# Leading bank, pinned weight splits, wide rotated chunks, and GpSimd lo parts in a two-block transformer

## The chip, the cores and the metric

The kernel runs on one core of a Trainium2 chip. The metric is the device time of one execution in microseconds, the median of several timed runs. One more execution was profiled; all profile rows come from it.

## The reference, cut to what matters

The input x has 256 tokens of width 1024. A first block (four token mixers, gates, an MLP of 4096) is followed by a retention layer with an FFN and by a native-sparse-attention (NSA) layer with an FFN. All of it is in float32. The change touches the products around these formulas:

```python
# retention, per head h (4 heads, q and k 256 wide, v 512 wide)
q, k = rotate_pairs(q, cos, sin), rotate_pairs(k, cos, sin) * (dk ** -0.5)
scores = einsum('bhid,bhjd->bhij', qc, kc) * intra_decay
o = einsum('bhij,bhje->bhie', scores, vc) + ...        # the state of the chunk before
o = o * rsqrt(mean(o * o) + eps);  out = (o * silu(g)) @ w_out
# NSA, shared keys and values
kc = silu(blocks(k_c + pe) @ w1_k) @ w2_k              # 15 blocks per group, hidden 256, width 64
vc = silu(blocks(v_c + pe) @ w1_v) @ w2_v
gate = sigmoid((x @ w_in)[..., 1024:])                 # 16 heads x 3 branches
o = gate0 * compressed + gate1 * selected + gate2 * window
# every layer
h = h + rms_norm(mixed);  normed = rms_norm(h);  h = h + rms_norm(swiglu_ffn(normed))
```

## The kernel before

Float32 products are made of three float32r products. A weight of 128x1024 (a *half*) is loaded into a raw tile (4 of them), ScalarE writes its rounded copy whi (L234), VectorE the rest, wlo = raw - whi (L237); activations are split the same way. `mm3` (L249 to L251) adds hi.hi, hi.lo and lo.hi in PSUM. Six buffers (WSP) hold halves, more where a stage opens a pool for its last ones. `ws_wide` (L274, L276) makes the same sum in two products: whi against x's hi and lo side by side (512 columns), and wlo against x's hi (256 columns); ScalarE then copies the second part (L277) and VectorE adds the first (L278). `ws_chunk` makes it with mm3 at 256 columns.

A layer ends in `project_back` (w_out, w_down, w_ro, w_fo, w_no): for each of two token halves t two PSUM banks of 512 columns are summed over all weight halves. The last six halves (last = 3 chunks of two) are *held*: t = 0 runs bank 0 over all of them and then bank 1, then `residual(0)` and `nxt.a(0)` (normalization of the rows: L406, L411, L414, a power on GpSimd at L416, L193 on VectorE and L194 on ScalarE) are written; then t = 1 runs, with `nxt.b(0)` (transposes L436, then hi and lo of the inputs at L209 and L210) ahead of the last held half. For w_out and w_no nk is 8, so six of the eight halves are held. The next layer starts with `an_groups`: eight halves (two groups of four), each used for t = 0 and, after `nxt.b(1)`, for t = 1; their wlo is made in two pieces of 512.

Tiles are placed and instructions ordered by a scheduler: on each engine it takes the first instruction in the order of the code that is ready by its own estimate, so a weight split far down can stand ahead of a residual, and products can change places. `issue_after` adds an edge that keeps an instruction behind a given one on the same engine.

Retention projects q and k of each head with ws_chunk (w_rqk, eight chunks), rotates them from PSUM (L1127 to L1130, the last sum on GpSimd), takes the scores of head h-1 after the q chunk of head h, and then for each of four groups runs `gates` (w_rg by `an_steps`, four halves) and `outputs`: at and v stay float32 there (L1164, L1166). NSA runs a list of steps, NSA_ORDER: K and Q are halves of the key and query projections, I0/I1 the inputs of the compressed keys and values (xs), H0/H1 their hidden layer (w_ck1, w_cv1, four halves each, L1366 and L1368), T, C the second layer, G and B the gate products, S and U the scores. `keep_queries` makes lo parts of the queries (L1338); `cmp_values` writes the values four times below each other (L1417) by 32 products of 32 rows.

## Time and profile before

| | us |
|---|---|
| median of 3 timed runs | 1207.35 (1204.04 to 1207.77) |
| profiled execution | 1208.24 |
| its span, first to last instruction | 1206.46 |

| engine | busy us | share |
|---|---|---|
| TensorE products | 1184.8 | 98% |
| TensorE weight loads | 1014.4 | 84% |
| VectorE | 806.3 | 67% |
| ScalarE | 662.9 | 55% |
| GpSimd | 80.8 | 7% |

PE is TensorE, PEld its weight loads, DVE VectorE, ACT ScalarE, POOL GpSimd, SP the queue that issues the loads. Products are pipelined and the ends of their records are modelled: records of 0.28 us that start 0.12 us apart take 0.12 us each. PEclk is the share of full speed that TensorE was granted. A float32 product shows as two records. "<-" behind an idle time names what ended it.

### The profile page before, as it was taken

The page shows a single profiled execution, that of the slowest core. Times are in us where ns is not written, and L with a number is a line of the kernel's source. Part 1 is how long each engine was busy: PE and PEld are TensorE (multiplying, and loading weights), DVE is VectorE, ACT ScalarE, POOL GpSimd, SP SyncE. Part 2 cuts the span into 40 slices and gives each one's busy share as a digit, 9 for nine tenths or more (in the row PEclk, how much of TensorE's full clock was granted, in tenths as well). Part 3 has the DMA queues.
Part 4 walks back from the last instruction along what each step waited for, and adds up shares of the span by engine and source line. Part 5 has one row for each costly group of instructions (what it writes and reads, how often), then busy time and mean ns, then how long its engine had stood idle before and what let it go on. Part 6 is the DMA issues. An engine that isn't in the chain of part 4 may idle for free.

```text
span 1206.5 us, 18129 instructions
## 1 busy us (share of the span) xinstructions
PE 1184.8 (98%) x6848; PEld 1014.4 (84%) x6848; DVE 806.3 (67%) x1413; ACT 662.9 (55%) x1148; POOL 80.8 (7%) x87
## 2 busy tenths in 40 slices
PE   8999999999999998999999999999999999999997
PEld 6999889887888887899878888888889877888886
DVE  7757877667746667557456665657778967655663
ACT  5545765655644454543555554556567876645561
POOL 1000001200000000012000000000100530000000
PEclk8999999999999999999999999999999999999999
DMA  7654454536455565554546355556655226555560
GB/s 239 196 175 158 140 191 158 175 126 230 161 192 187 191 208 181 177 194 158 166 148 213 120 192 189 192 185 212 209 194 179 72 70 205 179 189 186 189 205 35
DMA packets 60775, 210.11 MB, mean 174 GB/s; under 512 B 7120, under 2 KB 9808, under 8 KB 60560
## 3 DMA queue, kind: packets, MB, share of 16 engines
q1 hardware_dynamic: 60688, 208.95, 53.0%
q8 instruction: 54, 0.88, 0.3%
q14 instruction: 33, 0.27, 0.1%
HBM read 207.84 MB, written 1.08 MB: 173 GB/s over the span
## 4 chain that ended last, share of the span: by engine, by line
PE 82%; DVE 7%; DMA 5%; ACT 3%; issue 1%; POOL 0%; SPq 0%; DVEq 0%; POOLq 0%; ACTq 0%
PE b L274 19%; PE b L249 15%; PE b L251 15%; PE b L250 15%; PE b L276 9%; DVE wlo L237 3%; ACT whi L234 1%; PE b L436 1%; DMA raw<-w_up 1%; DMA raw<-w_no 1%; DMA raw<-w_rv 1%; PE b L1536 1%; DMA raw<-w_ck 1%; DMA wng<-w_ng 1%; ACT s L1503 1%
## 5 line engine op out<-in xcount | busy, mean ns | idle before, releaser
L237 DVE TENSOR_TENSOR wlo<-raw,whi 128x1024 fp32r<-128x1024 f32 (+3 forms) x432 | 470.9, 1103 | 265.1 <-ACT whi L234 262.2
L234 ACT ACTIVATE whi<-raw 128x1024 fp32r<-128x1024 f32 (+1 forms) x384 | 401.6, 1050 | 383.6 <-issue 116.5
L274 PE MATMUL b<-x,whi 128*128 128x512 f32 x1024 | 362.7, 398 | 0.0
L276 PE MATMUL b<-x,wlo 128*128 128x256 f32 x1024 | 286.3, 280 | 0.0
L249 PE MATMUL b<-whi,x 128*128 128x512 f32 (+1 forms) x720 | 283.9, 395 | 1.8 <-ACT x L209 1.0
L250 PE MATMUL b<-wlo,x 128*128 128x512 f32 (+1 forms) x720 | 280.7, 390 | 1.0 <-DVE wlo L237 0.8
L251 PE MATMUL b<-whi,x 128*128 128x512 f32 (+1 forms) x720 | 279.8, 390 | 0.6 <-DVE x L210 0.6
L274 PEld LDWEIGHTS b<-x,whi 128*128 128x128 f32 x1024 | 192.2, 188 | 45.9 <-issue 0.3
L276 PEld LDWEIGHTS b<-x,wlo 128*128 128x128 f32 x1024 | 193.1, 189 | 0.9
L249 PEld LDWEIGHTS b<-whi,x 128*128 128x128 f32 x720 | 136.1, 189 | 34.5 <-ACT x L209 4.3
L251 PEld LDWEIGHTS b<-whi,x 128*128 128x128 f32 x720 | 136.3, 189 | 29.9 <-DVE x L210 1.3
L250 PEld LDWEIGHTS b<-wlo,x 128*128 128x128 f32 x720 | 136.4, 189 | 28.7 <-DVE wlo L237 1.9
L249 PE MATMUL b<-x,whi 128*128 128x256 f32 x480 | 137.6, 287 | 0.0
L251 PE MATMUL b<-x,wlo 128*128 128x256 f32 x480 | 135.5, 282 | 0.4 <-DVE wlo L237 0.4
L250 PE MATMUL b<-x,whi 128*128 128x256 f32 x480 | 135.4, 282 | 0.0
L249 PEld LDWEIGHTS b<-x,whi 128*128 128x128 f32 x480 | 91.5, 191 | 2.1 <-issue 1.5
L251 PEld LDWEIGHTS b<-x,wlo 128*128 128x128 f32 x480 | 91.5, 191 | 0.6 <-DVE wlo L237 0.6
L250 PEld LDWEIGHTS b<-x,whi 128*128 128x128 f32 x480 | 91.6, 191 | 0.1
L416 POOL TENSOR_TENSOR rstd<-ms,mhalf 128x1 f32<-128x1 f32 x22 | 13.8, 626 | 686.5 <-DVE ms L414 686.5
L210 DVE SCALAR_TENSOR_TENSOR x<-b,gc,x 128x128 fp32r<-128x128 f32 x112 | 36.7, 348 | 20.2 <-ACT x L209 18.3
L209 ACT ACTIVATE x<-b,gc 128x128 fp32r<-128x128 f32 x112 | 37.9, 367 | 21.7 <-PE b L436 16.5
L1503 ACT ACTIVATE s<-s,nm 128x128 f32<-128x128 f32 (+1 forms) x64 | 28.2, 444 | 2.6 <-DVE rz L1507 1.4
(277 smaller groups left out, 1014.8 us busy)
## 6 DMA issues: line engine op xcount, KB each, us to landing
raw<-w_fi SPq DMA_DIRECT2D x88, 512.0 KB, 4.5
raw<-w_fo SPq DMA_DIRECT2D x44, 512.0 KB, 4.5
raw<-w_gate SPq DMA_DIRECT2D x32, 512.0 KB, 4.2
raw<-w_up SPq DMA_DIRECT2D x32, 512.0 KB, 3.9
raw<-w_down SPq DMA_DIRECT2D x32, 512.0 KB, 3.9
raw<-w_qk SPq DMA_DIRECT2D x24, 512.0 KB, 4.1
raw<-w_rv SPq DMA_DIRECT2D x16, 512.0 KB, 4.8
raw<-w_rqk SPq DMA_DIRECT2D x16, 512.0 KB, 4.5
```

The costliest lines, as they stand in the source:

```text
L209: k.nc.scalar.activation(hi, ps[:, j, :], AF.Copy, scale=g)
L210: k.nc.vector.scalar_tensor_tensor(lo, ps[:, j, :], g, hi.bitcast(F32), op0=OP.mult, op1=OP.subtract)
L234: nc.scalar.activation(hi[:, :n], r, AF.Copy)
L237: nc.vector.tensor_tensor(lo[:, c], r[:, c], hi[:, c].bitcast(F32), op=OP.subtract)
L249: mm(out, lhs[0], rhs[0], start=start, stop=False)
L250: mm(out, lhs[0], rhs[1], start=False, stop=False)
L251: mm(out, lhs[1], rhs[0], start=False, stop=stop)
L274: mm(ps.rearrange("p a t -> p (a t)"), half[0][:, s], x[2][:, k].rearrange("p a t -> p (a t)"), start=k == 0, stop=False)
L276: mm(ps[:, 0], half[1][:, s], x[0][:, k, :], start=False, stop=k == KT - 1)
L416: nc.gpsimd.tensor_tensor(r, ms, self.mhalf[:, :1], op=OP.pow)
L436: self.nc.tensor.transpose(ps[:, j, :], src[:, j * 128:(j + 1) * 128], self.ident)
L1503: nc.scalar.activation(s[:, a, i, :], s[:, a, i, :], AF.Exp, bias=nm[:, a, i:i + 1], scale=-1.0, accum_out=z[:, a, i:i + 1])
```

## The change

- `each_half` can make wlo on another engine; `cmp_hidden` makes the eight halves of the compressed layers on GpSimd, and `keep_queries` the lo parts of the queries.
- `an_groups` queues the splits of its third and later halves behind the last ScalarE and VectorE instructions of `nxt.a(0)` (*the pins*: `lasts`, `queued`, `rows_done`).
- `project_back`: where nk is 8, t = 0 (and t = 1 of a last layer) takes bank 0 of one held half ahead and then alternates the two banks.
- Retention: w_rqk by ws_wide, rotation from SBUF, the scores of head h-1 after the k chunk, those of the last head within the first gates; at and v are split into hi and lo (in the tiles of the rotation) and `outputs` multiplies by mm3.
- NSA: the gate weights are split after `an_groups`, the gate products come before H0, and `cmp_values` makes its four copies by 8 products, from an hT that GpSimd has copied four times.

```diff
-NSA_ORDER = ("Q0 K0 I0 H0 Q0 Q0 G I1 Q1 Q1 Q1 T0 K1 B C0 K1 K1 H1 K0 K0 "
+NSA_ORDER = ("Q0 K0 I0 G H0 Q0 Q0 I1 Q1 Q1 Q1 T0 K1 B C0 K1 K1 H1 K0 K0 "
...
-    def each_half(self, name, i, width=2048, pools=None, pieces=1):
+    def each_half(self, name, i, width=2048, pools=None, pieces=1, lo_on=None):
...
-                nc.vector.tensor_tensor(lo[:, c], r[:, c], hi[:, c].bitcast(F32), op=OP.subtract)
+                (lo_on or nc.vector).tensor_tensor(lo[:, c], r[:, c], hi[:, c].bitcast(F32), op=OP.subtract)
...
                 for j in range(4):
+                    queued = self.queued(self.rows_done if len(hs) > 1 else ())
                     if j % 2 == 0:
                         own = {s: pool for s in range(2) if len(hs) + s + extra >= 4 * len(groups)}
                         chunk = self.each_half(name, 2 * g + j // 2, 4 * n, own, 2)
-                    hs.append((i, 2 * j, next(chunk)))
+                    with queued:
+                        hs.append((i, 2 * j, next(chunk)))
...
+            lead = min(len(held), 1 if nk == KT else len(held))
             for t in range(2):
-                for banks in ((0,), (1,)) if t == 0 or not nxt else ((0, 1),):
-                    for a in held[:-1]:
-                        self.as_t(accs[t], *a, t, banks)
-                    if t and nxt:
+                if t == 0 or not nxt:
+                    order = [(i, 0) for i in range(lead)]
+                    for i in range(len(held)):
+                        order += [(i + lead, 0)] * (i + lead < len(held)) + [(i, 1)]
+                else:
+                    order = [(i, n) for i in range(len(held)) for n in range(2)]
+                for i, n in order:
+                    if t and nxt and (i, n) == (len(held) - 1, 0):
                         nxt.b(0)
-                    self.as_t(accs[t], *held[-1], t, banks)
+                    self.as_t(accs[t], *held[i], t, (n,))
                 residual(t, accs[t])
                 if nxt:
                     nxt.a(t)
+                    if t == 0:
+                        self.rows_done = self.lasts()
...
+    def lasts(self):
+
+        order = list(reversed(self.nc.cur_bb.bb.instructions))
+        return [next(i for i in order if i.engine == e.engine) for e in (self.nc.scalar, self.nc.vector)]
+
+    def queued(self, instructions):
+
+        es = ExitStack()
+        for i in instructions:
+            es.enter_context(self.tc.issue_after(i))
+        return es
...
-            def rotated(s, ps):
-                a = tp.tile([128, 2, T], F32, tag=f"rot{s}", name="rot")
+            def rotated(s, i):
+                a = self.ws_wide("w_rqk", i, xin, tp.tile([128, 2, T], F32, tag=f"rot{s}", name="rot"))
                 b = tp.tile([128, 2, T], F32, tag="rotb", name="rotb")
-                nc.vector.tensor_tensor(a, ps, cs, op=OP.mult)
                 for j in range(2):
-                    nc.vector.tensor_tensor(b[:, j, :], ps[:, 1 - j, :], sn[:, j, :], op=OP.mult)
+                    nc.vector.tensor_tensor(b[:, j, :], a[:, 1 - j, :], sn[:, j, :], op=OP.mult)
+                nc.vector.tensor_tensor(a, a, cs, op=OP.mult)
                 nc.gpsimd.tensor_tensor(a, a, b, op=OP.add)
...
-                    rot.append(rotated(s, self.ws_chunk("w_rqk", 2 * h + s, xin)))
-                    if s == 0 and qk:
+                    rot.append(rotated(s, 2 * h + s))
+                    if s == 1 and qk:
                         scores(h - 1, *qk)
...
+                    steps += 1
+                    if steps == 2 and g == 0:
+                        scores(3, *qk)
+                    if steps == (3 if g == 0 else 1):
+                        src = [v[:, t, g * 512:(g + 1) * 512] for t in range(2)] + [at[:, g, :]]
+                        for tag, x in zip(("rot0", "rot1", "rotb"), src):
+                            hl = [tp.tile([128, 2, T], F32, tag=tag, name=tag).rearrange("p a t -> p (a t)").bitcast(F32R)
+                                  [:, :x.shape[1]] for _ in range(2)]
+                            self.split(*hl, x)
+                            parts.append(hl)
+                return sg, parts
...
-                    mm(p, at[:, g, t * 128:t * 128 + 128], v[:, 0, vs], start=True, stop=t == 0)
+                    self.mm3(p, [x[:, t * 128:t * 128 + 128] for x in w], v0, True, t == 0)
                     if t:
-                        mm(p, at[:, g, T:384], v[:, 1, vs], start=False, stop=True)
+                        self.mm3(p, [x[:, T:384] for x in w], v1, False, True)
...
-            wg = tp.tile([128, KT, 96], F32R, name="wg")
-            self.split(wg[:, :, :48], wg[:, :, 48:], raw.rearrange("p (k c) -> p k c", k=KT))
...
+            wg = tp.tile([128, KT, 96], F32R, name="wg")
+            self.split(wg[:, :, :48], wg[:, :, 48:], raw.rearrange("p (k c) -> p k c", k=KT))
...
-                    nc.vector.tensor_tensor(lo, q[half[a], :, 128:], hi.bitcast(F32), op=OP.subtract)
+                    nc.gpsimd.tensor_tensor(lo, q[half[a], :, 128:], hi.bitcast(F32), op=OP.subtract)
...
-                    for u, (hi, lo) in enumerate(self.halves("w_c" + "kv"[s] + "1", c)):
+                    for u, (hi, lo) in enumerate(self.halves("w_c" + "kv"[s] + "1", c, lo_on=nc.gpsimd)):
...
+                for r in range(1, nr):
+                    nc.gpsimd.tensor_copy(hT[:, :, :, r, :15], hT[:, :, :, 0, :15])
...
-                for r in range(4):
-                    for g in range(4):
-                        for k in range(2):
-                            mm(p[r * 32:r * 32 + 32, g, :], hT[:, k, g, :], w2[:, 1, k, :], start=k == 0, stop=k == 1)
+                for g in range(4):
+                    for k in range(2):
+                        mm(p[:, g, :], hT[:, k, g].rearrange("p r n -> p (r n)"), w2[:, 1, k, :], start=k == 0,
+                           stop=k == 1)
```

## Rows read from the trace of the kernel before

**Rows 1.** Page of the profile: TensorE's busy time, share of the span, instructions.

```profile
PE 1184.8 (98%) x6848; PEld 1014.4 (84%) x6848; DVE 806.3 (67%) x1413; ACT 662.9 (55%) x1148; POOL 80.8 (7%) x87
```

**Rows 2.** TensorE timeline, 256-column and wide products: start, length, engine, line, shape.

```profile
559.99 0.28 PE L249 MATMUL b<-x,whi 128*128 128x256 f32 x1
...
560.35 0.28 PE L249 MATMUL b<-x,whi 128*128 128x256 f32 x1
...
729.98 0.40 PE L274 MATMUL b<-x,whi 128*128 128x512 f32 x1
...
730.33 0.39 PE L274 MATMUL b<-x,whi 128*128 128x512 f32 x1
```

**Rows 3.** TensorE timeline, outputs of one retention group and what follows.

```profile
587.91 1.88 PE L1164 MATMUL b<-v,at 128*128 128x512 f32 x4
...
590.72 0.39 PE L250 MATMUL b<-wlo,x 128*128 128x512 f32 x1
```

**Rows 4.** Timeline of TensorE and VectorE near the end of w_no.

```profile
995.80 0.47 PE L249 MATMUL b<-whi,x 128*128 128x512 f32 x1
...
997.04 0.50 PE L250 MATMUL b<-wlo,x 128*128 128x512 f32 x1 [0.76 <-DVE wlo L237]
...
998.54 1.22 DVE L237 TENSOR_TENSOR wlo<-raw,whi 128x1024 fp32r<-128x1024 f32 x1 [1.56 <-ACT whi L234]
...
998.56 1.03 PE L249 MATMUL b<-whi,x 128*128 128x512 f32 x2 [0.79 <-ACT whi L234]
...
1000.68 0.63 PE L250 MATMUL b<-wlo,x 128*128 128x512 f32 x1
```

**Rows 5.** TensorE timeline, held halves of w_out.

```profile
277.78 0.74 PE L249 MATMUL b<-whi,mx 128*128 128x512 f32 x2 [0.75 <-ACT whi L234]
```

**Rows 6.** Windows: length, PE, PEld, DVE, ACT, POOL busy, granted clock, DMA, GB/s.

```profile
477.30:480.00 2.70, 2.70 (x11) 2.51 (x12) 0.69 (x3) 1.06 (x4) 0.00 (x0) 0.50 0.00 0
...
999.00:1001.00 2.00, 2.00 (x6) 1.62 (x5) 1.75 (x3) 0.98 (x1) 0.00 (x0) 0.50 0.80 266
```

**Rows 7.** Timelines of VectorE and TensorE between w_down and retention.

```profile
469.98 1.29 DVE L237 TENSOR_TENSOR wlo<-raw,whi 128x512 fp32r<-128x512 f32 x2 [2.81 <-ACT whi L234]
...
477.28 1.94 PE L436 MATMUL b<-cm,xn 128*128 128x128 f32 x8 [3.34 <-DVE xn L193]
```

**Rows 8.** TensorE timeline, first products of the MLP.

```profile
292.38 0.50 PE L251 MATMUL b<-whi,x 128*128 128x512 f32 x1 [0.59 <-DVE x L210]
```

**Rows 9.** Windows from one normalization to the next transposes: retention, FFN, NSA, FFN.

```profile
477.14:489.03 11.89, 11.75 (x50) 9.95 (x51) 7.17 (x19) 5.50 (x15) 1.10 (x2) 0.88 0.30 110
676.02:689.38 13.36, 13.36 (x63) 10.73 (x62) 9.19 (x23) 7.49 (x19) 1.40 (x2) 1.00 0.17 43
863.04:874.98 11.94, 11.92 (x58) 9.59 (x56) 8.79 (x26) 7.74 (x24) 3.45 (x9) 1.00 0.59 164
1011.72:1024.31 12.59, 12.31 (x59) 9.79 (x58) 10.82 (x27) 8.78 (x20) 1.39 (x2) 1.00 0.48 162
```

**Rows 10.** Timelines of ScalarE and TensorE in NSA: gate split, first of H0.

```profile
877.60 0.52 ACT L242 ACTIVATE wg<-wng 128x384 fp32r<-128x384 f32 x1 [0.78 <-DMA wng<-w_ng]
...
903.18 0.38 PE L1366 MATMUL b<-whi,xs 128*120 128x256 f32 x1 [0.62 <-DVE xs L243]
```

**Rows 11.** Timelines of TensorE and GpSimd: the values, the first scores' multiplies.

```profile
937.73 3.18 PE L1417 MATMUL b<-w,hT 128*32 128x64 f32 x64
...
939.37 2.22 POOL L1509 TENSOR_TENSOR s<-s,rz 128x512 f32<-128x512 f32 x2 [0.83 <-DVE rz L1507]
```

**Rows 12.** Timelines of GpSimd and VectorE: an add alone, a split during an add.

```profile
189.00 1.29 POOL L937 TENSOR_TENSOR macc<-macc,g 128x512 f32<-128x512 f32 x1 [33.49 <-DVE g L936]
...
557.79 2.12 DVE L237 TENSOR_TENSOR wlo<-raw,whi 128x1024 fp32r<-128x1024 f32 x1
```

**Rows 13.** Windows in the rotated chunks and in NSA, columns as above.

```profile
525.00:575.00 50.00, 50.00 (x407) 49.53 (x406) 32.89 (x41) 18.04 (x18) 12.54 (x7) 1.00 0.53 171
...
900.00:925.00 25.00, 24.38 (x211) 24.06 (x210) 21.03 (x33) 16.26 (x25) 0.31 (x1) 1.00 0.56 187
```

More of the change, by code (lines that the diff above doesn't have):

```diff
@@ L489, in run @@
             self.ps = self.pool(es, "ps", 8, bass.MemoryType.PSUM)
+            self.rows_done = ()
             nc.scalar.preload_act_table_set("natural_log_exp_and_others")
@@ L1152, in gates, with outputs @@
                 sg = tp.tile([128, 2, 512], F32, tag="sg", name="sg", bufs=1)
+                parts, steps = [], 0
                 for _ in self.an_steps("w_rg", g, 512, xin,
                                        lambda t, ps: nc.scalar.activation(sg[:, t, :], ps, AF.Silu)):
-                    pass
-                return sg
-            def outputs(g, sg):
-                vs = slice(g * 512, (g + 1) * 512)
+                    steps += 1
[9 more added lines that the diff above has]
+                return sg, parts
+            def outputs(g, sg, parts):
+                v0, v1, w = parts
                 ss = self.st.tile([128, 2], F32, tag="ss2", name="ss2")
@@ L1186, in retention @@
                 sg = gates(g)
-                if g == 0:
-                    scores(3, *qk)
-                else:
+                if g:
                     transposed(yn)
-                yn = outputs(g, sg)
+                yn = outputs(g, *sg)
             e1.close()
@@ L1388, in cmp_hidden, with cmp_transposed @@
                 return folded("hd", 60, parts)
-            def cmp_transposed(hd):
+            def cmp_transposed(hd, nr):
                 p = unfolded(hd, 60, 0)
@@ L1405, in cmp_keys @@
                     for k in range(2):
-                        mm(p[u * 64:u * 64 + 64, :], w2[:, 0, k, :], hT[:, k, :, :15], start=k == 0, stop=k == 1)
+                        mm(p[u * 64:u * 64 + 64, :], w2[:, 0, k, :], hT[:, k, :, 0, :15], start=k == 0, stop=k == 1)
                 for u in range(2):
```

8 lines of the change are left out of this document (5 added, 3 removed).

## The prediction

> **What bounds the kernel now.** I read the page first. TensorE is busy for 98% of the span [rows 1], and the granted clock is full in nearly every slice, so a microsecond is won either by giving TensorE less to stream or by closing a place where its next product starts late. A record's length does not price a product, since records overlap. The step from one start to the next does, so I read the TensorE timeline of each stage by steps. A float32r product of 256 columns steps by 0.12 us, a wide pair (512 and 256 columns) by about 0.35 us [rows 2], and a 512-column product by 0.23 us (the step in [rows 4] wherever nothing waits). Places where a step is longer are the whole stock of stalls. They lie at the seams between layers, not inside them: the end of w_no [rows 4], the end of w_out [rows 5], the seam from w_down to retention [rows 7], the one from w_out to the MLP [rows 8], and a few places in NSA [rows 10]. Then I read the windows of VectorE behind each seam [rows 9] and in the middle of the stages [rows 13], because four parts of the change move work to, from or along that engine.
>
> **The change, part by part.** All sums are made against the profiled execution, 1208.24 us (span 1206.46), which lies 0.9 us above the median of the three timed runs, 1207.35.
>
> *Retention, the rotated chunks.* Eight chunks of w_rqk have 16 k-steps each. Three products of 256 columns (0.36) become a wide pair (0.345 to 0.35) [rows 2]: 128 x 0.010 to 0.015 = 1.3 to 1.9 us less, I take **1.6**. Each chunk adds two ScalarE copies and two VectorE adds. In 525 to 575 us VectorE is busy 32.89 of 50 and ScalarE 18.04 of 50 [rows 13]; an add of 128x256 is a quarter of a lo part's 1.22 us [rows 4] and some overhead, 0.4 us, so two per chunk of 6 us bring VectorE to about 80%, and the chain runs beside the next chunk's products. If that cover were gone, it would cost 8 x 0.8 = 6.4 us.
>
> *Retention, the outputs.* Per group, three float32 products of 512 columns are six records, from 587.91 to 590.49 (the next layer's second product at 590.72 less one step of 0.23): 2.58 us [rows 3]. Nine float32r products at 0.23 take 2.06. Four groups give **2.1** less. The twelve added splits (about 0.65 us each on ScalarE and on VectorE) wait for the previous readers of the rot tiles and block ScalarE's queue there, with the weight splits of later steps behind them. Two converted halves, 5.5 us of TensorE work, are then still ahead, and three splits with one weight take about 3 us: hidden. The scores of a head stand one chunk later, with nothing waiting for them.
>
> *The leading bank in w_no.* TensorE runs bank 0 of all six held halves first and eats one half per 0.69 us, faster than one is made. It waits 1.24 - 0.23 = 1.01 us at 997.04 and 0.95 us at 998.56 [rows 4], and then nine steps run at 0.42 to 0.43 instead of 0.23 (five of them from 998.56 to 1000.68 [rows 4]), since the granted clock is 0.50 of full speed, 1.2 GHz [rows 6]: 1.8 us. Together 3.8 us. With the new order a half is eaten every 1.37 us. At 995.80 four such bank steps of 0.69 are done; in the new order the last held half is the tenth, so it is wanted five steps later, at 999.25, and its lo part 0.23 after that. The lo part is ready at 998.54 + 1.22 = 999.76 [rows 4]. A wait of 0.3 to 0.4 remains: **3.4** less. The first bank is now complete 1.4 us before the second instead of 4.1, which is still enough for its square sum to be done ahead.
>
> *The leading bank in w_out.* One wait of 0.75 idle (0.91 against the step) for a hi part [rows 5], and some 0.4 in slow steps around it. In the new order the last held half is wanted about 2 us later, so all goes: **1.3** less.
>
> *The pins.* From the third half on, a stage's weight splits are put behind the normalization of token half 0 on ScalarE and on VectorE. What goes: before retention VectorE stood 2.81 us idle behind a hi part, made late, then split it for 1.29, and only then added the second bank of the residual, which was long complete; TensorE idled 3.34 us until 477.28 [rows 7], and the 2.7 us after that ran at 1.2 GHz [rows 6], half of it lost: 3.34 + 1.35 = 4.7. Before the MLP the lo part of the inputs came late behind weight splits, 0.59 idle [rows 8], with its neighbours 1.7. What comes: four halves that used to be split early now fall into the window between that normalization and the second transposes, eight pieces of 0.65 us (two took 1.29 [rows 7]), 5.2 us of VectorE. In the four windows of [rows 9] VectorE's work grows from 7.17 to 12.4 of 11.89 (retention), from 9.19 to 14.4 of 13.36 (first FFN), from 8.79 to 14.0 of 11.94 (NSA), and from 10.82 to about 14.0 of 12.59 (second FFN, where part of these pieces stands in the window already). At the MLP there is room. If VectorE were filled without a gap, the overflow is 5.0 us; at the best filling that these rows show, 10.82 of 12.59 or 86%, it is 14.0. In the two FFN stages the last half is wanted only after the second transposes, which takes 1.2 off each: 2.6 to 11.6, and I take the middle, 7.0. So the pins cost 7.0 and give back 6.4: **+0.6**, from -3.8 to +5.2. The loads on SP's queue are not pinned, but a pinned half holds its raw tile.
>
> *NSA.* The gate split waited for its weights, 0.78 us of ScalarE at 877.60, in front of the inputs' hi parts [rows 10]; moved behind, it gives **0.65**. H0 waited 0.62 us for xs [rows 10], 0.78 by steps; the gate products (16 at 0.12, 1.9 us) now stand there and cover it: **0.7**. The values' 64 records, 3.1 us [rows 11], become 16 with four times the columns of weights. If a record keeps its step, 2.3 us less; but the transposes behind it wait for the two GpSimd multiplies that end at 941.59 [rows 11], so it may be nothing. I take **0.5**, near the end that the row of the follower sets. Eight lo parts of 128x1024 move from VectorE (1.22 us [rows 4]) to GpSimd. A 128x512 add there takes 1.29 us [rows 12], so one of these takes 2.6. The parts are made some halves ahead, but the last of H0 and of H1 are made close before use, and come up to 1.4 us later each: 0 to 2.8, I take **+1.0**. The queries' lo parts (eight of 64x256) leave VectorE where it is full and stand among GpSimd's multiplies: -1.5 to +1.5, taken at **-0.3**. NSA together: -1.2.
>
> A VectorE split that met a GpSimd add took 2.12 us instead of 1.22 [rows 12]: the two did not overlap, the second waited for the first. The Trainium skill, SBUF — State Buffer, "Who interferes with whom", gives this as an exclusive lock: a VectorE instruction with two SBUF inputs and a GpSimd instruction that reads SBUF block one another for the whole instruction. By that rule, with which the trace agrees, the moved lo parts free VectorE of nothing for its other splits; this speaks against the change, and the port rival below has its price from rows.
>
> Sum: -1.6 - 2.1 - 3.4 - 1.3 + 0.6 - 1.2 = -9.0 us. From the profiled 1208.24 that is 1199.2, from the median 1198.35; I say **1198.5**.
>
> **The rivals.**
> *The pins are nearly free* (VectorE is filled without gaps): 4.4 less again, 1194. For it: gaps exist in the windows. Against: the work there comes in chains that wait on each other.
> *The planner already had the order.* The order on an engine comes from the scheduler, which swaps ready products; in w_out it went on to other products while a lo part was missing. If it does so whatever the order in the code, the leading bank gives nothing: 4.7 back, 1203. Against it: w_no plainly waited twice.
> *The port.* Eight lo parts hold the shared path for 8 x 2.6 = 20.6 us instead of 8 x 1.22 = 9.8. VectorE has 4.0 us free in 900 to 925 [rows 13]; the other 6.8 us of the 10.8 would reach TensorE: 1205.
> *Slower: the pinned splits starve the seams.* Four raw tiles hold the pinned halves, so the loads behind them start only after the normalization. If at each of the four seams a lo part then waits for a load as it did once before (2.81 us [rows 7]) and the clock falls as it did twice (1.8 us [rows 6]), that is 4 x 4.6 = 18.4 us: 1217. It decides once the waits at the four seams sum to over 16 us. Against it: the first four halves are loaded well before.
>
> **How the numbers follow.** Chances: forecast 0.50, pins free 0.08, planner 0.14 (1203), port 0.15 (1205), starved seams 0.13 (1217). A measurement of this kernel can tell about 0.3%, 3.6 us, from no change, so faster means below 1203.7: most of the forecast, the free pins and half of the planner, 0.61. Within 0.3% lie the rest of these and the port, 0.25. Slower: 0.14. The range reaches from 1192 (free pins and NSA 2 us better) to 1208, past the port case with the pins somewhat dearer; it leaves out the starved seams and little below.
>
> **What would show it.** In w_no, no step above 0.7 us and no stretch at 1.2 GHz. In retention, the float32 outputs gone and each group 0.5 us shorter. Before retention, the residual's second add directly behind its bank, and the 3.34 us gone. Waits of 1 to 3 us before the second transposes in retention, the FFNs and NSA, for lo parts or for the second normalization, are the pins' price; none would make the forecast too high. If NSA grows between H0 and the first scores, it is the port. The prediction is wrong if the seams' waits sum to more than 16 us or if w_no still stalls.

## The result and the profile after

| | before | after |
|---|---|---|
| median of the timed runs, us | 1205.88 (1204.04 to 1207.77, 4 runs) | 1216.88 (1215.27 to 1220.28, 4 runs) |
| ratio, 95% interval | | 1.0092 (1.0068 to 1.0117) |
| profiled execution, us | 1208.24 | 1216.58 |

The changed kernel is slower by 0.9%; the forecast was 1198.5, 0.7% faster, and the time lies outside its range. The kernel before was timed again beside each group of experiments, and its median moved between 1205.88 and 1207.99, so all comparisons below go by the ratio to the kernel before as timed beside the run; 0.001 is 1.2 us.

Where the time went is read from the starts of the same products in both TensorE timelines (the first transposes of each layer, the transposes of the compressed inputs, the first scores of the second kind): the shift of the start, after less before, and how it grows from one to the next.

| stretch | forecast | measured | shift at its end |
|---|---|---|---|
| up to the end of w_out | -1.3 | -1.4 | -1.4 |
| seam to the MLP | with the pins | +1.0 | -0.4 |
| seam to retention | with the pins | -2.1 | -2.5 |
| retention, rotated chunks / outputs | -1.6 / -2.1 | -0.9 / -1.8 | -5.2 |
| seam to the first FFN | with the pins | +2.2 | -3.0 |
| first FFN and seam to NSA, until the keys' projection ends | with the pins | +6.2 | +3.2 |
| rest of NSA | -1.2 (all its terms) | +4.2 | +7.4 |
| w_no | -3.4 | -3.6 | +3.9 |
| seam to the second FFN | with the pins | +3.8 | +7.7 |
| rest | 0 | +0.7 | +8.3 |
| all pins (the five seams) | +0.6 | +11.1 | |

So the stretches of w_out, w_no and retention came nearly as forecast, and two things went wrong: the seams, and NSA. The -3.6 of w_no is not the leading bank's alone, though. TensorE timelines of the kernel before and of the kernel before with the pins alone (an experiment below), the ends of this stretch:

```profile
956.40 0.38 PE L1490 MATMUL b<-kT,qT 64*128 64x128 f32 x2
...
1011.86 0.38 PE L436 MATMUL b<-cm,xn 128*128 128x128 f32 x2
```

```profile
961.79 0.38 PE L1507 MATMUL b<-kT,qT 64*128 64x128 f32 x2
...
1014.75 0.49 PE L440 MATMUL b<-cm,xn 128*128 128x128 f32 x3
```

It takes 55.46 us before and 52.96 with the pins alone: 2.5 of the 3.6 come without a leading bank. So the pins' account is the five seams less this gain. The rows for what came as forecast first: the outputs of a retention group, in the TensorE timeline after (they answer [rows 3]).

```profile
584.64 0.39 PE L249 MATMUL b<-rot,rotb 128*128 128x512 f32 x1
...
586.69 0.39 PE L249 MATMUL b<-whi,x 128*128 128x512 f32 x1
```

Nine products take 586.69 - 584.64 = 2.05 us, as forecast; in w_no, from 995.4 us on, no bank step is above 0.24 us.

Now the windows from each first normalization's transposes to the second's, of the kernel after (columns as in [rows 9], which they answer: retention, first FFN, NSA, second FFN):

```profile
473.42:486.56 13.14, 12.28 (x51) 8.02 (x49) 11.68 (x28) 8.85 (x19) 1.72 (x2) 1.00 0.61 216
672.09:685.53 13.44, 12.94 (x56) 8.79 (x54) 11.70 (x28) 9.52 (x21) 1.08 (x2) 1.00 0.42 130
860.75:872.72 11.97, 11.31 (x49) 7.88 (x48) 11.97 (x33) 9.40 (x25) 3.89 (x9) 1.00 0.79 228
1015.72:1030.97 15.25, 13.51 (x55) 8.82 (x54) 11.73 (x28) 11.99 (x24) 1.39 (x2) 1.00 0.35 111
```

The third column from the left after the length (VectorE) rose by 4.5, 2.5, 3.2 and 0.9 us against [rows 9]: the pinned pieces stand in these windows, as the prediction said. What it did not see stands behind the third window. ScalarE and TensorE timelines of the kernel after, then a window of it:

```profile
877.78 0.52 ACT L242 ACTIVATE wg<-wng 128x384 fp32r<-128x384 f32 x1 [3.56 <-DMA wng<-w_ng]
...
878.61 0.80 PE L249 MATMUL b<-whi,x 128*128 128x512 f32 x1 [3.18 <-ACT x L209]
```

```profile
877.50:884.50 7.00, 5.89 (x15) 4.65 (x15) 3.37 (x9) 4.45 (x10) 0.00 (x0) 0.52 0.16 55
```

The gate split, now written behind the layer's first products, was still placed by the scheduler among the inputs' hi parts (L209), and waited 3.56 us there for its load; TensorE waited 3.18, and then ran at half clock (the window has 0.52 of full speed, 1.2 GHz but for its edges). Of these 7 us it worked 5.89; half speed cost it 5.89 x 0.48 = 2.8 us more. Why the load was late stands on SP's queue, timeline after, and in a window by its DMA share (second column from the right; the last is GB/s):

```profile
835.79 27.72 SPq L231 DMA_DIRECT2D raw<-w_kv  x8
863.56 0.43 SPq L1312 DMA_DIRECT2D tz<-rbrows  x1
864.04 5.02 SPq L1314 DMA_DIRECT2D pe<-c_pe  x1
...
870.55 0.43 SPq L1320 DMA_DIRECT2D wng<-w_ng  x1
```

```profile
852.00:862.00 10.00, 10.00 (x50) 8.39 (x49) 5.00 (x11) 4.50 (x8) 1.08 (x2) 1.00 0.01 2
```

For ten microseconds nothing is loaded at all: the raw tiles are held by halves whose split must wait for the normalization at 859. Then the rest of w_kv, the 2 MB of tz and four small loads, the gate weights last, go out together, and the gate weights land 7.2 us after their issue.

The second loss is in NSA. Timelines of VectorE, GpSimd and TensorE after, between the hidden layer of the keys and their second layer, and the window behind:

```profile
913.64 4.57 DVE L237 TENSOR_TENSOR wlo<-raw,whi 128x1024 fp32r<-128x1024 f32 x2
918.13 3.32 DVE L243 TENSOR_TENSOR xs<-xf,xs 128x960 fp32r<-128x960 f32 x1
921.38 0.74 DVE L1429 TENSOR_SCALAR hs<-hs 128x120 f32<-128x120 f32 x1
...
914.37 6.06 POOL L237 TENSOR_TENSOR wlo<-raw,whi 128x1024 fp32r<-128x1024 f32 x2 [6.96 <-ACT whi L234]
920.51 1.53 POOL L1371 TENSOR_TENSOR whi<-qT,whi 64x256 fp32r<-64x256 f32 x1
...
922.55 0.70 PE L1444 MATMUL b<-hT,w 128*64 128x60 f32 x8 [3.10 <-DVE hT L1434]
```

```profile
922.00:929.00 7.00, 6.45 (x36) 6.33 (x37) 2.67 (x6) 0.50 (x1) 3.12 (x3) 0.53 0.50 178
```

While GpSimd makes two lo parts, VectorE's split of xs takes 3.32 us. The small sum that hT needs (hs) is queued behind it; TensorE waits 3.10 for hT and then again runs at half clock, 6.45 us of work at 0.53, which costs another 3.0.

### The profile page after: what moved, and what is told of

Same layout as the page of the kernel before. It is cut to its first block, busy times and chain, and to the rows that moved or that the text cites. A ratio compares the mean times of both kernels' runs of the same rounds, so it can differ in the third digit from the quotient of the medians.

```text
span 1214.8 us, 17871 instructions
## 1 busy us (share of the span) xinstructions
PE 1188.3 (98%) x6684; PEld 1008.4 (83%) x6684; DVE 812.7 (67%) x1425; ACT 670.3 (55%) x1176; POOL 108.5 (9%) x106
## 4 chain that ended last, share of the span: by engine, by line
PE 79%; DVE 9%; DMA 4%; ACT 4%; issue 2%; SPq 1%; POOL 1%; DVEq 0%; POOLq 0%; ACTq 0%
PE b L274 22%; PE b L249 13%; PE b L250 13%; PE b L251 13%; PE b L276 11%; DVE wlo L237 3%; ACT s L1541 2%; DMA raw<-w_fi 1%; DMA raw<-w_up 1%; ACT whi L234 1%; PE b L446 1%; POOL rstd L426 1%; DMA wng<-w_ng 1%; PE b L1574 1%; DMA res<-x 1%
## 5 line engine op out<-in xcount | busy, mean ns | idle before, releaser
L237 DVE TENSOR_TENSOR wlo<-raw,whi 128x1024 fp32r<-128x1024 f32 (+3 forms) x424 | 462.0, 1104 | 252.5 <-ACT whi L234 249.4
L274 PE MATMUL b<-x,whi 128*128 128x512 f32 x1152 | 408.0, 398 | 0.0
L274 PEld LDWEIGHTS b<-x,whi 128*128 128x128 f32 x1152 | 216.3, 188 | 51.7 <-issue 0.3
L249 PEld LDWEIGHTS b<-whi,x 128*128 128x128 f32 x720 | 136.3, 189 | 40.3 <-ACT x L209 12.4
L249 PE MATMUL b<-x,whi 128*128 128x256 f32 x352 | 102.3, 291 | 0.0
L250 PE MATMUL b<-x,whi 128*128 128x256 f32 x352 | 100.3, 285 | 0.0
L249 PEld LDWEIGHTS b<-x,whi 128*128 128x128 f32 x352 | 68.0, 193 | 2.1 <-issue 1.5
L250 PEld LDWEIGHTS b<-x,whi 128*128 128x128 f32 x352 | 68.1, 194 | 0.1
L209 ACT ACTIVATE x<-b,gc 128x128 fp32r<-128x128 f32 x112 | 37.3, 364 | 12.8 <-PE b L446 8.2
```

Of the source, the lines that this page charges most:

```text
L209: k.nc.scalar.activation(hi, ps[:, j, :], AF.Copy, scale=g)
L237: (lo_on or nc.vector).tensor_tensor(lo[:, c], r[:, c], hi[:, c].bitcast(F32), op=OP.subtract)
L249: mm(out, lhs[0], rhs[0], start=start, stop=False)
L250: mm(out, lhs[0], rhs[1], start=False, stop=False)
L274: mm(ps.rearrange("p a t -> p (a t)"), half[0][:, s], x[2][:, k].rearrange("p a t -> p (a t)"), start=k == 0, stop=False)
```

## The experiments

### What the pins cost

The changed kernel without pins, and the kernel before with the pins alone:

```diff
-                    queued = self.queued(self.rows_done if len(hs) > 1 else ())
+                    queued = self.queued(())
```

> The changed kernel without the pins (the splits of the third and later halves of a layer's first products are free again); all else stays. Theory A, the pins hold four raw tiles, so that no load runs for some 10 us before NSA and the gate weights come late (3.34 us of waiting at 875.04, then 3.42 us lost at half clock), and they cost 2.4 and 3.9 us at the two FFN seams and 1.0 at the MLP, against 2.1 us won before retention: 6.1 + 2.4 + 3.9 + 1.0 - 2.1 = 11.3 us less than the changed kernel, about 1205.6, and the wait before the second half of NSA's inputs is under 1 us. Theory B, the pins are innocent of the wait at NSA (the gate split stands in front of the inputs and waits for its load anyway): 5.2 us less, about 1211.7, with a wait of 3 us or more still at that place. Theory C, the pins bring on balance what they were forecast to cost, nothing: 1216 to 1218.

Measured: 1208.47, ratio 1.0008 (0.9997 to 1.0019). The change with pins was 1.0092, so they cost 0.0084, 10.1 us; theory A holds in kind and nearly in size.

> The kernel before with the pins alone. Theory A, they cost 2.4 + 3.9 at the FFN seams and 1.0 at the MLP and win 2.1 before retention, and in NSA, where the gate split is still written ahead of the inputs, anything from 0 to 6.1: 1211 to 1217, slower than before. Theory C, they cost as much as they bring (as forecast, +0.6): 1205 to 1208.

Measured: 1214.99, 1.0068 (1.0047 to 1.0088), 8.2 us: theory A. Theory C, the forecast's, is out in both. The gate split waited 4.80 us there. SP's queue in the kernel without pins (first its waits between 835 and 885 us, the columns being total, times, longest; then its timeline), and the same wait of the kernel after:

```profile
SPq L231 <- DVE wlo L237: 32.1, 13, 10.6
```

```profile
837.94 12.38 SPq L231 DMA_DIRECT2D raw<-w_kv  x7
...
862.64 1.74 SPq L1314 DMA_DIRECT2D pe<-c_pe  x1
...
865.70 0.44 SPq L1320 DMA_DIRECT2D wng<-w_ng  x1
```

```profile
SPq L231 <- DVE wlo L237: 40.2, 11, 15.1
```

The longest stop of the queue falls from 15.1 to 10.6 us, the load of w_kv is issued in 12.4 us (seven of eight) instead of 27.7, and the gate load goes out at 865.70 instead of 870.55. The windows of the kernel without pins show what the pinned pieces themselves cost:

```profile
475.09:487.17 12.08, 12.08 (x51) 9.94 (x52) 7.18 (x19) 5.25 (x15) 1.10 (x2) 0.86 0.30 109
672.67:684.77 12.10, 12.10 (x58) 9.77 (x57) 9.18 (x23) 7.26 (x18) 1.40 (x2) 1.00 0.19 49
859.76:870.35 10.59, 10.59 (x52) 8.54 (x50) 8.77 (x26) 7.50 (x23) 3.45 (x9) 1.00 0.60 179
1011.20:1023.75 12.55, 12.25 (x57) 9.74 (x58) 11.25 (x27) 8.64 (x20) 1.40 (x2) 1.00 0.51 169
```

Against the kernel after, the four stretches are 1.06, 1.34, 1.38 and 2.70 us shorter: 6.5 in sum. By place, the shifts of the two kernels give for the pins +1.5 at the MLP, -2.1 at retention, +2.2 at the first FFN, +5.7 before NSA, +1.2 over w_no and the second FFN's seam (-2.5 and +3.7), +0.4 elsewhere: 8.9 between the two profiled executions.

Is it the held raw tiles or the work stacked up behind the normalization? Three kernels asked this. First, pins from the fifth half on:

```diff
-                    queued = self.queued(self.rows_done if len(hs) > 1 else ())
+                    queued = self.queued(self.rows_done if len(hs) > 3 else ())
```

> The changed kernel with the pins from the fifth half on instead of the third; all else stays. Four halves are pinned, as many as there are raw tiles, so the eight loads can all be issued and nothing of the loads behind them waits for a raw tile but the next layer's. Theory A, the loss before NSA is the loads held up on SP's queue: the queue is free some 10 us sooner, the gate split waits under 1.5 us instead of 3.6, and NSA's 6.3 us come back, with some 2 of the FFN seams' too: 1208 to 1210. Theory B, the loss is the pinned work itself on VectorE and ScalarE behind the normalization: a third less of it, 1212 to 1215, and the gate split still waits 2 us or more.

Measured: 1209.65, 1.0017 (1.0008 to 1.0026). The pins of the third and fourth half, a third of the pinned work, carry 0.0075 of the 0.0084. That speaks for the tiles: with four pinned halves for four raw tiles the w_kv loads go out in 15.09 us. The time is A's, but A's other number fell: the gate split still waited 2.34 us, as B had it, and TensorE 1.94 for the inputs behind it. Second, the gate load ahead of the others:

```diff
+            raw = tp.tile([128, KT * 48], F32, name="wng")
+            nc.sync.dma_start(raw, I["w_ng"])
             tz = cp.tile([128, 16, T], F32, name="tz")
...
-            raw = tp.tile([128, KT * 48], F32, name="wng")
-            nc.sync.dma_start(raw, I["w_ng"])
```

> The whole changed kernel, pins included; only the load of the gate weights stands ahead of the 2 MB load of tz on SP's queue instead of behind it and three small ones. Theory A, the wait of 3.34 us at 875.04 (and the 3.42 lost at half clock behind it) hangs on this load alone, which the pins let be issued some 5 us later: the wait falls below 1 us and the time by 5 to 6.7, to about 1211. Rival, something else of the pinned work is late right behind it (hi and lo of the inputs, the second normalization): a wait of 2 us or more stays there, 1214 to 1217.

Measured: 1213.99, 1.0060 (1.0042 to 1.0078), 3.9 us less than the change by the ratios, whose intervals overlap: the rival. ScalarE and TensorE timelines:

```profile
870.95 0.53 ACT L242 ACTIVATE wg<-wng 128x384 fp32r<-128x384 f32 x1 [3.31 <-DMA wng<-w_ng]
...
875.46 0.80 PE L250 MATMUL b<-wlo,x 128*128 128x512 f32 x1 [2.20 <-DVE wlo L237]
```

Issued at 864.6, the load still landed 6.4 us later, beside the late w_kv loads; the split, now placed further ahead, held up ScalarE for 3.31 us, and pinned lo parts came late in turn. Third, two more raw tiles in the two FFN stages:

```diff
+            raws = self.pool(es, "ar_" + groups[0][0], 2) if groups[0][0] in ("w_fi","w_fi00","w_fi10") else None
...
-                        chunk = self.each_half(name, 2 * g + j // 2, 4 * n, own, 2)
+                        chunk = self.each_half(name, 2 * g + j // 2, 4 * n, own, 2, raws=raws if len(hs) == 2 else None)
```

> The whole changed kernel with every pin, with two more raw tiles in the two FFN stages alone, for the third and the fourth half of their first products. Theory A, the pins cost because pinned halves hold the four raw tiles, so that the loads of the seventh and eighth half start only behind the normalization: with six raw tiles all eight are loaded before it, the seams before the two FFNs get 1.4 and 3.1 us shorter (to what they were with the pins from the fifth half on), 1212 to 1213. Theory B, it is the twelve pieces of splits stacked up on VectorE behind the normalization, wherever their raw tiles are: the two seams stay within 0.7 us, 1215.5 to 1217.5.

Measured: 1220.12, 1.0105 (1.0087 to 1.0123): slower than either theory, though not told from the change's 1.0092. The new tiles' space was not free: SP's queue (waits between 650 and 690 us) stood still for them until the layer's last products.

```profile
SPq L231 <- PE b L251: 18.2, 1, 18.2
```

Their loads went out at 674.82, behind the first transposes; TensorE then waited 1.67 us for a hi part at 680.26, and the seam to the first FFN cost 5.0 us instead of 2.2. So at this seam, with the same pinned work, later loads cost more, but the stacked work was not tried alone. At the second FFN it is plain in the ScalarE and TensorE timelines of the kernel after: three released hi parts run ahead of the inputs'.

```profile
1015.81 2.94 ACT L234 ACTIVATE whi<-raw 128x1024 fp32r<-128x1024 f32 x3
1018.65 0.34 ACT L209 ACTIVATE x<-b,gc 128x128 fp32r<-128x128 f32 x1
...
1019.05 0.50 PE L249 MATMUL b<-whi,x 128*128 128x512 f32 x1 [0.84 <-ACT x L209]
```

### What GpSimd's lo parts cost

The eight lo parts back on VectorE, with the pins and without:

```diff
-                    for u, (hi, lo) in enumerate(self.halves("w_c" + "kv"[s] + "1", c, lo_on=nc.gpsimd)):
+                    for u, (hi, lo) in enumerate(self.halves("w_c" + "kv"[s] + "1", c)):
```

> The changed kernel with the eight lo parts of the compressed layers back on VectorE; all else stays. Theory A, GpSimd's adds hold up VectorE's splits (one of xs took 3.32 us at 918.13 while an add ran on GpSimd), which makes hT late: the wait of 3.27 us in front of the compressed keys and the 3.42 us lost at half clock behind it go, about 1210.2, and the split of xs takes under 2 us. Theory B, VectorE is full there and hT comes late whoever makes the lo parts: 1215 to 1218 and the wait in front of the compressed keys stays above 2 us.

Measured: 1214.25, 1.0053 (1.0033 to 1.0072): 4.7 us less than the change by the ratios, whose intervals just overlap. The direction is A's, and so is the split of xs, at 1.15 us; the wait that stayed in front of the compressed keys, 2.28 us, is B's.

> The changed kernel without the pins and with the lo parts of the compressed layers on VectorE: what is left is retention, the leading bank, the gate order, the queries' lo parts on GpSimd and the values in 8 products. Theory A, the two losses are separate and add up: 1216.9 - 11.3 - 6.7 = 1198.9, faster than the kernel before by 0.6%. Rival, the two losses share a cause (a late start of NSA), so that taking both away gives only the larger one: about 1205.

Measured: 1204.44, 0.9973 (0.9961 to 0.9986). The lo parts cost 0.0035, 4.2 us, here too, so the two losses add up, but the time is the rival's: something was left. VectorE, GpSimd and TensorE timelines of this kernel:

```profile
914.08 1.63 DVE L1429 TENSOR_SCALAR hs<-hs 128x120 f32<-128x120 f32 x1
...
913.15 1.59 POOL L1371 TENSOR_TENSOR wlo<-qT,wlo 64x256 fp32r<-64x256 f32 x1
914.68 0.95 POOL L1433 MEMSET hT<- 128x1024 f32 x1
...
916.19 0.46 PE L1444 MATMUL b<-hT,w 128*64 128x60 f32 x8 [2.28 <-POOL hT L1433]
```

The queries' lo parts on GpSimd now stand where the large ones stood: hs takes 1.63 us. The memset of hT is queued behind them on GpSimd and ends at the same time as hs, so this run does not say which of the two TensorE would have waited for alone. Without them too:

```diff
-                    nc.gpsimd.tensor_tensor(lo, q[half[a], :, 128:], hi.bitcast(F32), op=OP.subtract)
+                    nc.vector.tensor_tensor(lo, q[half[a], :, 128:], hi.bitcast(F32), op=OP.subtract)
```

> The changed kernel without the pins and with all lo parts (compressed layers and queries) on VectorE; the gates' new place stays. Theory A, the queries' lo parts on GpSimd make hT late (the sum in front of hT took 1.63 us instead of 0.22 while GpSimd worked): the wait in front of the compressed keys falls below 0.5 us, about 1200.5. Rival, the gates' new place does it, as it takes TensorE work away from between H0 and the compressed keys: the wait stays above 1.5 us, 1203 to 1205.

Measured: 1203.04, 0.9964 (0.9950 to 0.9978). The wait falls to 0.57 us: A's mechanism; but the time is the rival's, since w_no of this kernel ends in a wait of 2.79 us for the first normalization. Last, the large lo parts on GpSimd alone, on a kernel with retention, the leading bank and the values in 8 products only (below):

```diff
-                    for u, (hi, lo) in enumerate(self.halves("w_c" + "kv"[s] + "1", c)):
+                    for u, (hi, lo) in enumerate(self.halves("w_c" + "kv"[s] + "1", c, lo_on=nc.gpsimd)):
```

> Retention, leading bank and values in 8 products (1202.5), with the eight lo parts of the compressed layers on GpSimd and nothing else there; gates at their old place. Theory A, GpSimd's adds hold up VectorE's splits by themselves: xs or a lo part on VectorE takes over 2 us, H0 or the compressed keys wait over 1.5 us, 1205 to 1207. Rival, it costs only together with the queries' lo parts or the gates' new place: 1202 to 1203.5.

Measured: 1209.36, 1.0016 (1.0002 to 1.0029), against 0.9959 without them: 6.9 us. Theory A, and more. VectorE, GpSimd and TensorE timelines, and under them the same VectorE lines of the kernel without:

```profile
915.11 2.56 DVE L1370 TENSOR_TENSOR wlo<-qT,wlo 64x256 fp32r<-64x256 f32 x1
...
915.04 2.34 POOL L237 TENSOR_TENSOR wlo<-raw,whi 128x1024 fp32r<-128x1024 f32 x1 [0.24 <-PE b L251]
...
918.36 0.46 PE L1443 MATMUL b<-hT,w 128*64 128x60 f32 x8 [3.08 <-DVE hT L1433]
...
948.28 0.38 PE L251 MATMUL b<-x,wlo 128*128 128x256 f32 x1 [2.40 <-DVE wlo L237]
```

```profile
908.89 1.16 DVE L243 TENSOR_TENSOR xs<-xf,xs 128x960 fp32r<-128x960 f32 x1 [0.47 <-ACT xs L242]
...
911.94 0.42 DVE L1370 TENSOR_TENSOR wlo<-qT,wlo 64x256 fp32r<-64x256 f32 x1
912.40 0.22 DVE L1428 TENSOR_SCALAR hs<-hs 128x120 f32<-128x120 f32 x1
```

A split of 0.42 us became one of 2.56 under one GpSimd add of 2.34, and TensorE waited 3.08 for hT behind it. The Trainium skill, SBUF — State Buffer, "Who interferes with whom", says that whoever issues first gets the shared ports for the whole instruction and the other is blocked; the rows agree, 2.56 being close to 2.34 + 0.42. The second wait, 2.40 against 0.40 in the kernel without, stands 22 us behind the last of the GpSimd lo parts, and the split it waits for took its usual 1.22 us (from 947.00); that these 2.0 of the 6.9 us come from the lo parts by another way is not shown.

### What the rest is worth

Three parts alone (no pins, nothing on GpSimd, gate split and gate products at their old place), and, second diff, the same with the pins before retention:

```diff
-NSA_ORDER = ("Q0 K0 I0 G H0 Q0 Q0 I1 Q1 Q1 Q1 T0 K1 B C0 K1 K1 H1 K0 K0 "
+NSA_ORDER = ("Q0 K0 I0 H0 Q0 Q0 G I1 Q1 Q1 Q1 T0 K1 B C0 K1 K1 H1 K0 K0 "
```

```diff
-                    queued = self.queued(())
+                    queued = self.queued(self.rows_done if len(hs) > 1 and groups[0][0] == "w_rv" else ())
```

> The kernel before with three parts of the change alone: retention, the leading bank, the values in 8 products; no pins, nothing on GpSimd, gate split and gate products where they were. Theory A, what NSA still loses without the pins and with the large lo parts on VectorE (the 2.52 us in front of the compressed keys and 1.71 at half clock) comes from the queries' lo parts on GpSimd and the gates' new place: 1204.4 - 4.2 = 1200.2. Rival, that wait comes from the values' new hT or from retention's earlier start: about 1204 with the wait still there. In both, w_no ends in a wait of 1.5 to 2 us in front of the first transposes, for the normalization that the longer alternation of the banks leaves less time.

> The same as the run before it, with the pins in front of retention alone, the one seam where they won (2.1 us). Theory A, the seams do not act on each other: 2.1 less than without these pins, about 1198. Rival, what is won there is lost at the next seam, since the loads stand later from then on: no difference.

Measured: 1202.54, 0.9959 (0.9945 to 0.9972), and 1201.35, 0.9950 (0.9937 to 0.9963). In the first the wait before the compressed keys is gone (theory A), though less was won than A said; the second wins 1.1 us more, which the intervals do not tell from nothing. Retention alone, then the leading bank alone, on the kernel before; of the change's diff these are the parts in `rotated`, `gates`, `outputs` and their callers, and the part in `project_back`:

```diff
-                    rot.append(rotated(s, self.ws_chunk("w_rqk", 2 * h + s, xin)))
+                    rot.append(rotated(s, 2 * h + s))
...
-                yn = outputs(g, sg)
+                yn = outputs(g, *sg)
```

> The kernel before with the change of retention alone. The forecast's terms are 1.6 for the rotated chunks and 2.1 for the outputs; the traces show 1.0 and 1.8 in the stage: 2.8 to 3.7 less than the kernel before, 0.9969 to 0.9977 of it. Rival, the scheduler's order changes at other seams by as much as in the other kernels (1 to 2 us either way) and hides it: 0.998 to 1.000.

Measured: 1203.70, 0.9979 (0.9969 to 0.9989), 2.5 us, at the end of A's span; the stage itself is 2.7 us shorter, as in the kernel after.

```diff
+                    order = [(i, 0) for i in range(lead)]
+                    for i in range(len(held)):
+                        order += [(i + lead, 0)] * (i + lead < len(held)) + [(i, 1)]
```

> The kernel before with the leading bank alone. The forecast gave it 4.7 us (3.4 in w_no, 1.3 in w_out): 1203. Theory A, it wins only 1 to 1.5 in each, as a new wait of 1.3 to 1.5 us stands in front of the first transposes behind w_no (the first bank is complete 1.4 us ahead of the second instead of 4.1, and its square sum is no longer done ahead): 1204.5 to 1205.5.

Measured: 1207.14, 0.9996 (0.9984 to 1.0008): nothing, below both. In its TensorE timeline w_out and w_no are shorter by 1.6 and 1.9, the second already less a new wait of 1.59 for the normalization behind it. Other waits grew: before retention's first transposes (3.34 in [rows 7], with half clock for 7 us behind it instead of 3.5) and at the end of the first FFN.

```profile
475.17 1.94 PE L441 MATMUL b<-cm,xn 128*128 128x128 f32 x8 [3.64 <-DVE xn L193]
...
852.55 0.50 PE L249 MATMUL b<-whi,x 128*128 128x512 f32 x1 [1.22 <-ACT x L242]
...
1011.22 1.09 PE L441 MATMUL b<-cm,xn 128*128 128x128 f32 x8 [1.59 <-DVE xn L193]
```

### A faster kernel

The kernel with pins before retention alone, with the gate load ahead of tz as above:

> Retention, leading bank, values in 8 products and the pins in front of retention alone (1201.35), and the load of the gate weights ahead of the one of tz. Theory A, the wait of 1.0 to 1.35 us before the second half of NSA's inputs goes: 1200.2. Rival, the inputs are no earlier than the gate split was, so no difference: 1201 to 1202.

Measured: 1199.45, 0.9933 (0.9919 to 0.9947), theory A: no wait is left before the second half of NSA's inputs. This is faster than the kernel before and the kernel after; against 0.9950 without the moved load the intervals overlap. Taking the leading bank out of it:

```diff
-                if t == 0 or not nxt:
-                    order = [(i, 0) for i in range(lead)]
...
+                for banks in ((0,), (1,)) if t == 0 or not nxt else ((0, 1),):
```

> The kernel of 1199.45 (retention, values in 8 products, pins before retention alone, gate load first) without the leading bank. Theory A, the leading bank is worth nothing in any kernel, since what it wins at the ends of w_out and w_no is waited for in front of the next transposes: 1199 to 1200.5. Rival, it is worth what w_out and w_no show in the traces without pins, 1.6 + 1.3 to 1.9, and its zero alone came from losses elsewhere (the clock before retention, the end of w_fo0): 1202 to 1203.

Measured: 1200.59, 0.9954 (0.9938 to 0.9970): 2.5 us by the ratios, 1.1 by the medians, with intervals that overlap. The two traces do not show the 2.5: the bank takes 1.3 us off w_out and nothing off w_no (54.20 us with it, 54.05 without), and the profiled execution without it is the shorter one, 1200.66 against 1201.21. Three variations (bank 0 three halves ahead; the retention pins from the fifth half; both):

```diff
-            lead = min(len(held), 1 if nk == KT else len(held))
+            lead = min(len(held), 3 if nk == KT else len(held))
...
-len(hs) > 1 and groups[0][0] == "w_rv"
+len(hs) > 3 and groups[0][0] == "w_rv"
```

> The kernel of 1199.45 (retention, leading bank, values in 8 products, pins before retention alone, gate load first) with bank 0 three held halves ahead of bank 1 in w_out and w_no instead of one. Theory A, the leading bank's gain in w_no is taken back by the wait for the first normalization (1.57 us in front of the transposes at 1002.90): with the first bank complete 2.7 us before the second instead of 1.4 the wait falls below 0.5, and 0.7 to 1.0 us are won: 1198.6. Rival, the halves then come late again (0.8 us at 993.31 becomes 1.5 or more): no difference or slower, 1199.5 to 1200.5.

> The kernel of 1199.45 with the pins before retention from the fifth half on instead of the third. Theory A, the third and the fourth pinned half cost more than they bring, since the raw tiles held by them stop the loads: that seam won 2.8 us with the pins from the fifth half and 1.5 with those from the third, so 1.3 less: 1198.2. Rival, the pins of the third and fourth are the ones that free VectorE for the residual: 1 us or more is lost, 1200.5.

> The lead of three halves and the pins before retention from the fifth half together, on the kernel of 1199.45. If both win and do not act on each other: 1197.3. If only one does, about 1198.3; if the scheduler's order elsewhere decides, within 1 us of 1199.45.

Measured: 0.9942 (0.9925 to 0.9959), 0.9937 (0.9920 to 0.9953) and 0.9932 (0.9918 to 0.9947). None can be told from 0.9933. With three halves of lead the wait behind w_no did fall, from 1.41 to 0.66 us idle, without showing in the time.

## Why the prediction was wrong

Taken back one part after another, the ratios are 1.0092 (all), 1.0008 (no pins), 0.9973 (large lo parts on VectorE), 0.9964 (queries' too), 0.9959 (gates back), in us: pins 10.1, lo parts 4.2, queries 1.1, gates 0.6, and 4.9 won by what is left. The intervals tell the first two from nothing, and the last; not the queries' and the gates' steps. Against the steps of the prediction:

- **The pins** are the step that failed: +0.6 was forecast (-3.8 to +5.2), 8 to 10 measured. Its cost term, 7.0 us of VectorE work in four windows, came out near in size, 6.5 between the windows with and without pins, but in part by luck: VectorE's work there rose by 11.1 us, where 18.8 were forecast, and ScalarE's by 10.2 (5.50 to 8.85, 7.49 to 9.52, 7.74 to 9.40, 8.78 to 11.99), which the term did not price. The largest of the four differences, 2.70 at the second FFN, stands where VectorE works 11.73 of 15.25 us and TensorE was seen waiting for ScalarE. Two things were missing. The prediction saw that "a pinned half holds its raw tile" and went no further along SP's queue: behind the held w_kv loads stand tz, three small loads and the gate weights, and the gate split sits in ScalarE's queue ahead of the inputs. That is 5.7 us before NSA, 5.0 of them the wait (3.18 us against 0.98 without pins) and the half clock behind it (2.8). And of the 6.4 to be given back, the MLP's 1.7 turned into a loss of 1.0 to 1.5, while retention's 4.7 gave 2.1 net. The rival of the starved seams named this mechanism; that its 1217 is the measured time is luck. It put the pins at 18.4 us in four equal waits, where the runs show 8 to 10, one large wait and smaller ones; GpSimd's lo parts and terms that did not come made up the rest.
- **GpSimd's lo parts**: +1.0 was taken from a span of 0 to 2.8; they cost 4.2 to 6.9. The mis-sized step counted how much later GpSimd's own result comes; TensorE waited for one of those once in the kernel after, 0.47 us. What came late was VectorE's work: the splits and sums in whose way the adds stood, hT above all. The port rival's 6.8 us was the right size by luck: the loss came not from a lack of VectorE time but from held instructions in front of hT, and from the clock behind that wait.
- **The queries' lo parts**: -0.3 forecast, about 1 lost by the ratios, which their intervals do not tell from nothing, and within the forecast's own bound of 1.5. The row of hs (1.63 us for 0.22) shows a mechanism for it.
- **Gate split and gate products**: 0.65 and 0.7 forecast, neither came. Moving the split in the code did not move it behind the inputs: without pins TensorE still waits 0.98 there. And before H0 the scheduler put one half of the queries' projection less, so that the gate products took its place instead of adding cover; the wait for xs is 0.42 to 1.0 us in the kernels with the new order, 0.62 before.
- **The values**: 0.5 forecast. Sixteen records take 1.9 us instead of 3.2, but in the kernel with three parts alone the transposes behind them then wait 0.69 and 0.53 for GpSimd's multiplies: about 0.2 is left. The prediction had named these multiplies as what could leave nothing.
- **Retention**: right in mechanism; 2.7 instead of 3.7. The rotated chunks won 0.92 (49.97 to 49.05 us), since a wide pair steps 0.007 below three products, not 0.010 to 0.015; the outputs 1.8 to 2.1.
- **The leading bank**: in w_out it came as forecast (-1.4). In w_no the -3.6 matches the forecast by luck: the pins alone give 2.5 there (no stretch at half clock is left in it, and the longest step is 0.86 us), and the changed kernel without pins, bank included, 1.0. Alone the bank is worth nothing. The stalls of [rows 4] belonged to that one order of the splits: with retention's change alone, without any leading bank, w_no is 1.6 us shorter as well. Where nothing pins the splits, the bank's gain is waited for again in front of the transposes, since the first bank is no longer complete early (the prediction held 1.4 us to be enough).
- **The chances**: slower was given 0.14, on "the first four halves are loaded well before". The two rivals that cost time were taken as alternatives, and both came in part.

Not settled: how the pins' price divides between late loads and the work stacked on ScalarE and VectorE at the FFN seams.

## What to carry to other kernels

A pin on a split is a pin on its buffer: follow the loading queue past the held tiles to every small load behind them, and ask who waits for each, before pricing the pinned work itself. Before moving work to GpSimd, look not at its own deadline but at what VectorE has to finish while it runs. And a stall seen in one order of a scheduled kernel is worth its length only in that order: count on it only if the edge that makes it survives.

## What the runs showed of the hardware

- GpSimd and VectorE gained next to nothing side by side in one stretch of the kernel after: from 914.37 to 921.45 two adds on GpSimd (2.40 undisturbed, at 886.92 in the kernel with the large lo parts on GpSimd alone) and two VectorE splits (1.22 [rows 4] and 1.16 alone) together took 7.1 us, their sum being 7.2; the last 0.5 us of a third split lie in it too.
- VectorE sums with one input in PSUM (the inputs of the compressed layers, 64x240) were not held: in the kernel with the large lo parts on GpSimd alone eight of them took 3.34 us from 892.76 on, 0.4 each, beside a GpSimd add that took 2.40; in the kernel after, with GpSimd idle, they took 3.34 from 910.27 on.
- A one-input VectorE sum (hs) was held as well, 1.63 us for 0.22, beside a GpSimd add and a memset, and ended 0.08 us behind the memset. The Trainium skill, SBUF — State Buffer, "Who interferes with whom", has a scalar-operand instruction contend with GpSimd only in a two-port mode; whether it ran in one, no row here shows.
- Waits of 3.18 and 3.10 us were each followed by 7 us at half clock and cost 2.8 and 3.0 us on top, nearly their length again. The slow stretch does not go by the length of the wait: 2.28 us (large lo parts back on VectorE, pins kept) was also followed by 7 us, but 3.08 (large lo parts on GpSimd alone) and 4.42 (pins alone) by 3.4.
- The issue of the small load behind tz took 5.02 us on SP's queue in the kernel after, where loads of w_kv issued just before it were still on their way, and 1.74 in the kernel without pins, where none were.
